# First part of a fused two-branch residual block: four unread products ahead of the first transposes, the first weight's rounding moved from ScalarE to VectorE, and two projections placed next to each other

## The chip, the cores and the metric

The kernel runs on one core of one Trainium2 chip. The metric is the device time of one execution in microseconds (us). The kernel before took 925.51 us, the median of three runs that lie between 925.22 and 925.88.

## The reference

The block normalises 1040 rows (16 learned rows ahead of 1024 frames, 1024 wide), projects them with one wide matrix, runs two branches on slices of the projection, merges them through gates, projects the result and normalises again. Cut to what matters here:

```python
h = concat([meta, x])                      # 1040 rows of 1024, padded
u = rmsnorm(h, norm_g)                     # what the first part forms
proj = u @ w_in                            # 1024 x 6144; its first pieces are formed in the first part
(sb_q, sb_k, sb_v, sb_gate, hg_q, hg_f, hg_i, hg_gate, gate_sb, gate_hg) = split(proj)
y_sb = stick_breaking(sb_q, sb_k, sb_v) * silu(sb_gate)
y_hg = group_rmsnorm(hgrn2(hg_q, hg_f, hg_i, lb)) * silu(hg_gate)
h = h + (sigmoid(gate_sb) * (y_sb @ w_sb_out) + sigmoid(gate_hg) * (y_hg @ w_hg_out)) @ w_out
out = rmsnorm(h, final_norm_g)[16:1040]
```

## The kernel before

Every operand of a large product is kept as two rounded parts, a high part and a low part that holds what the rounding left, and a product is formed as high x high + low x high + high x low. `uh` and `ul` are the two parts of the normalised rows, transposed so that channels lie on the partitions; `wh` and `wl` those of a weight of 1024 x 128.

The change lies in the first part. It takes the rows in nine blocks of 128 (the last has 16), brings each into `uh` and `ul`, and between them forms projections for three of the four `hg_i` weights, in pieces of 256 columns (the last 272). All instructions of ScalarE, VectorE and TensorE in this part stand in an order that is written out by hand, a table of short step names that is worked off from left to right; each engine then runs its own instructions strictly in that order. GpSimd and the SyncE queue, which issues the loads, follow their program order and wait on semaphores. The steps, with the engine and the line of the profile:

- `S b`: sum of squares of block b (ScalarE, L169). `r b`: its inverse root (GpSimd, L175). `D b`: the block scaled (VectorE, L181; in two halves for blocks 0 and 1).
- `T b k`: four transposes of 128 x 128 of half k of block b (TensorE, L189), into one of two buffers in PSUM called `tr` for even b, or of two called `z` for odd b.
- `H b k`: rounds that half into `uh` (ScalarE, L198). `L b k`: the low part into `ul` (VectorE, L202). `R b k`: an unrounded copy into `xb` (ScalarE, L208). A buffer in PSUM is free again when its H, L and R are done, so `T30` waits for `R10`, `T50` for `R30`, `T60` for `R40`.
- `w i`: the high parts of weight i, four instructions of 128 x 256 (ScalarE, L330). `v i c`: a quarter of its low parts (VectorE, L335).
- `P i q`: the piece q of projection i, 24 products (TensorE, L345): eight of `uh` with `wh`, eight of `ul` with `wh`, eight of `uh` with `wl`. Piece 0 needs blocks 0 and 1, piece 1 blocks 2 and 3, and so on. `E i q`: its copy out of PSUM (ScalarE, L315) and a store issued on ScalarE's queue (L316).
- `X`, `Y`, `y`, `Z`: later sums of the blocks (VectorE and ScalarE, L219 to L222 and L353 to L361).

After the table comes the fourth `hg_i` projection (L259, products of 348 and 346 columns), and after that everything else.

Of the kernel before, what the change touches and what calls it, by code (L numbers as in the profile page):

```python
# [9 lines left out]
F32R = mybir.dt.float32r  # L10
# [5 lines left out]
P = 128  # L16
D = 1024
NC = D // P
SEQ = 1024
NM = 16  # L20
L = SEQ + NM
# [6 lines left out]
SH = 2  # L28
# [17 lines left out]
def block_kernel(ctx: ExitStack, tc: tile.TileContext, x, meta, norm_g, w_in, w_sb_out,  # L46
                 w_hg_out, w_out, hg_norm_g, hg_lb_logits, final_norm_g, out):
    nc = tc.nc
    V, S, G, T = nc.vector, nc.scalar, nc.gpsimd, nc.tensor
# [5 lines left out]
    def nm(s):  # L55
        uid[0] += 1
        return f"{s}_{uid[0]}"
# [7 lines left out]
    def sb(tag, shape, dt=F32):  # L65
        p = base if tag in HOME else here[-1]
        return p.tile(shape, dt, tag=tag, name=nm(tag), bufs=BUFS.get(tag, 1))

    def ps(tag):
        return psum.tile([P, 512], F32, tag=tag, name=nm(tag), bufs=PB[tag])  # L70
# [7 lines left out]
    ident = sb("ident", [P, P])  # L78
# [14 lines left out]
    def fetch_w(src, col, chunks):  # L93
        if chunks > NC // 2:
            raw = sb("wr", [P, NC, P])
        else:
            if not half_rows:
                t = sb("wl", [P, 2, NC // 2, P])
                half_rows.extend((t[:, 0], t[:, 1]))
            half_rows.reverse()  # L100
            raw = half_rows[0]
        nc.sync.dma_start(raw[:, :chunks], src[:, col:col + P].rearrange("(c p) n -> p c n", p=P))
        return raw
# [30 lines left out]
    start = ExitStack()  # L134
# [11 lines left out]
    w3 = SUM[4][0].rearrange("p (a c) (d n) -> p a (c d) n", a=2, n=P)  # L146
    xbs, raws, eps_x = [], [], []
# [175 lines left out]
    first_w = {}  # L323

    def high_w(i):
# [3 lines left out]
        for c in range(0, NC, SH):  # L329
            S.activation(h[:, c:c + SH], raw[:, c:c + SH], AF.Copy)  # L330

    def low_w(i, c):
        h, lo = first_w[i]
        cs = slice(c * SL, c * SL + SL)
        V.tensor_tensor(lo[:, cs], raws[i][:, cs], h[:, cs].bitcast(F32), op=ALU.subtract)  # L335
        if c == 3 and i == 0:
            raws.append(fetch_w(w_in[0], FIRST[2], NC))
# [21 lines left out]
    def further_low(b, k):  # L359
        src, h, low, ts = FURTHER[b, k]  # L360
        formed["low"] = V.tensor_tensor(low[:, :, ts], src, h[:, :, ts].bitcast(F32), op=ALU.subtract)  # L361


    STEPS = dict(S=stats, r=root, D=scaled, T=turned, H=high_part, L=low_part, R=whole, w=high_w, v=low_w, P=piece, E=kept_piece, X=further,
                 Y=further_high, y=further_high_s, Z=further_low)
    with tc.manual_schedule(engines={mybir.EngineType.Activation, mybir.EngineType.DVE, mybir.EngineType.PE}):
        for step in """
            S0 S1 w0 r0 D0 T00 H00 r1 T01 H01 D1 T10 H10 L00 T11 H11 S2 R00 L01 R01 S3 w1
            L10 L11 v00 v01 v02 v03 P00 r2 D2 T20 H20 r3 T21 H21 R10 R11 S4 D3 v10 v11 v12 v13
            P10 L20 T30 H30 L21 T31 H31 E00 R20 R21 S5 E10 w2 r4 D4 L30 L31 P01 v20 T40 H40 v21  # L370
            T41 H41 E01 R30 R31 S6 v22 P11 v23 r5 D5 T50 H50 L40 T51 H51 S7 E11 R40 L41 P20 R41
            r6 D6 T60 H60 L50 T61 H61 E20 R50 L51 P21 R51 S8 E21 r7 P02 D7 T70 H70 X0 T71 H71
            Y02 P12 Z02 L60 R60 L61 R61 E02 r8 D8 T80 H80 X1 T81 H81 Y12 P22 Z12 L70 R70 L71 R71
            L80 R80 L81 P03 R81 E12 E22 y01 y11 E03 X2 P13 y21 Y22 P23 Z22 X3 y31 Y32 Z32 X4 y41
            E13 y03 y13 E23 y23 y33 y43 y04 y14 y24 y34 y44 Y42 Z42 Z01 Z11 Z21 Z31 Z41 Z03 Z13 Z23
            Z33 Z43 Z04 Z14 Z24 Z34 Z44
            """.split():
            STEPS[step[0]](*(int(n) for n in step[1:]))
    lbl = sb("lbl", [P, 2, 4])
# [647 lines left out]
    for p in range(4):  # L1027
        for hh in range(2):
            u = [Unit(pairs[p][0], hh, g, g % 2) for g in range(4)]
# [270 lines left out]
```

## Time and profile before

| what | value |
|---|---|
| median of three runs | 925.51 us |
| the profiled execution | 926.64 us |
| its span, first to last instruction | 924.9 us |
| TensorE busy in the span | 899.3 us (97%) |
| VectorE, ScalarE, GpSimd busy | 659.2, 397.3, 267.8 us |
| the first part: first product of the table to first product of L259 | 8.07 to 57.57 us |

Rows of the timeline give the start in us, the duration, the engine, the line, the operation, what is written and read, how many instructions were merged, and in brackets how long the engine had stood idle before and what ended that. Rows of stretches give for each engine the busy time in the stretch. A matmul's record overlaps the next one, so the distance between starts is the pace and the duration of a merged row is a little longer than what it occupies.

### The profile page before, as it was taken

How to read it: one execution, taken by the hardware profiler on the slowest of the kernel's cores; microseconds unless marked ns; L12 is line 12 of the kernel's file. 1: busy time of each engine (PE TensorE's matmuls, PEld its weight loads, DVE VectorE, ACT ScalarE, POOL GpSimd, SP SyncE). 2: the span in 40 equal slices, each digit the busy share in tenths (PEclk: the TensorE clock that was granted, in tenths of full speed). 3: DMA queues.
4: the chain of work that ended last, by engine and by line, in shares of the span. 5: the costliest groups of instructions: out<-in, count | busy, mean ns of one | idle time of the engine just before them, and what ended most of it. 6: DMA issues, size and time to landing. Idle time of an engine off the chain costs nothing.

```text
span 924.9 us, 13722 instructions
## 1 busy us (share of the span) xinstructions
PE 899.3 (97%) x5000; PEld 781.8 (85%) x5000; DVE 659.2 (71%) x1205; ACT 397.3 (43%) x909; POOL 267.8 (29%) x285
## 2 busy tenths in 40 slices
PE   7999999999999999999999999999999999999996
PEld 6998888888889998898898888898978888888885
DVE  6893456554423477888788788868687887997886
ACT  6763334333333455555555555232324154323341
POOL 2026445544432211132111221424332000003552
PEclk9999999999999999999999999999999999999999
DMA  8223543333336122221141132131111347564212
GB/s 275 65 68 102 169 137 103 125 106 122 103 126 188 53 81 79 69 69 58 58 115 57 58 92 85 43 102 58 58 57 47 103 142 268 187 224 156 94 46 92
DMA packets 90581, 98.03 MB, mean 106 GB/s; under 512 B 6017, under 2 KB 65281, under 8 KB 90514
## 3 DMA queue, kind: packets, MB, share of 16 engines
q1 hardware_dynamic: 76688, 73.52, 26.0%
q10 hardware_dynamic: 13826, 23.64, 6.9%
q8 instruction: 40, 0.66, 0.3%
q14 instruction: 27, 0.22, 0.1%
HBM read 71.94 MB, written 25.20 MB: 105 GB/s over the span
## 4 chain that ended last, share of the span: by engine, by line
PE 80%; DVE 10%; ACT 4%; issue 2%; DMA 2%; POOL 1%; SPq 0%; ACTq 0%; DVEq 0%; POOLq 0%
PE acc L259 31%; PE acc L461 10%; PE z L461 7%; PE tr L461 7%; PE acc L1227 4%; PE av L677 3%; PE z L833 3%; PE tr L663 2%; PE z L621 2%; PE z L1227 2%; PE tr L1227 2%; PE acc L345 2%; DVE ab L630 2%; DVE ab L626 1%; DMA wr<-in_w_in 1%
## 5 line engine op out<-in xcount | busy, mean ns | idle before, releaser
L259 PE MATMUL acc<-uh,wh 128*128 128x346 f32 (+2 forms) x472 | 173.4, 367 | 0.0
L259 PE MATMUL acc<-uh,wl 128*128 128x346 f32 (+2 forms) x472 | 165.4, 350 | 0.0
L259 PE MATMUL acc<-ul,wh 128*128 128x346 f32 (+2 forms) x472 | 165.2, 350 | 0.0
L120 POOL TENSOR_TENSOR wl<-wr,wh 128x256 fp32r<-128x256 f32 x92 | 74.9, 836 | 300.4 <-ACT wh L115 272.8
L259 PEld LDWEIGHTS acc<-uh,wl 128*128 128x128 f32 x472 | 89.0, 189 | 6.0
L259 PEld LDWEIGHTS acc<-uh,wh 128*128 128x128 f32 x472 | 89.2, 189 | 3.6
L259 PEld LDWEIGHTS acc<-ul,wh 128*128 128x128 f32 x472 | 89.4, 189 | 2.5
L450 POOL TENSOR_TENSOR pw<-su,pw 128x512 fp32r<-128x512 f32 x44 | 59.2, 1366 | 44.2 <-ACT pw L449 44.0
L623 ACT ACTIVATE ab<-z 128x456 f32<-128x456 f32 (+6 forms) x112 | 49.9, 448 | 30.6 <-PE z L621 30.3
L450 POOL TENSOR_TENSOR pw<-wr,pw 128x512 fp32r<-128x512 f32 x33 | 43.7, 1325 | 61.2 <-ACT pw L449 61.2
L666 DVE TENSOR_TENSOR wt<-tr,wt 128x512 fp32r<-128x512 f32 (+1 forms) x80 | 50.4, 631 | 13.9 <-ACT wt L665 12.2
L626 DVE TENSOR_TENSOR_SCAN ab<-ab,later 128x456 f32<-128x456 f32 (+3 forms) x64 | 54.8, 858 | 6.8 <-ACT ab L623 6.1
L461 PE MATMUL acc<-th,pw 128*128 128x512 f32 x176 | 58.1, 391 | 0.0
L677 PE MATMUL av<-wt,v 128*128 128x256 f32 x320 | 53.9, 287 | 3.6 <-DVE wt L666 2.0
L665 ACT ACTIVATE wt<-tr 128x512 fp32r<-128x512 f32 (+1 forms) x80 | 44.2, 554 | 29.3 <-PE tr L663 29.0
L621 PE MATMUL z<-stk,q 128*128 128x456 f32 (+6 forms) x224 | 56.7, 334 | 0.0
L842 DVE COPY_PREDICATED ab<-mask,z 128x192 f32<-128x192 uint8 (+2 forms) x144 | 45.2, 352 | 13.0 <-PE z L833 11.6
L677 PEld LDWEIGHTS av<-wt,v 128*128 128x128 f32 x320 | 46.9, 188 | 8.4 <-DVE wt L666 3.7
L630 DVE TENSOR_TENSOR_SCAN ab<-ab 128x348 f32<-128x348 f32 (+4 forms) x48 | 46.9, 976 | 7.6 <-ACT ab L623 6.2
L449 ACT ACTIVATE pw<-su 128x512 fp32r<-128x512 f32 x44 | 25.8, 625 | 60.9 <-DVE su L444 36.8
L663 PE MATMUL tr<-ident,ab 128*128 128x128 f32 x288 | 45.0, 273 | 0.0
L115 ACT ACTIVATE wh<-wr 128x256 fp32r<-128x256 f32 x92 | 33.8, 411 | 26.0 <-issue 15.2
(348 smaller groups left out, 2107.1 us busy)
## 6 DMA issues: line engine op xcount, KB each, us to landing
wr<-in_w_in SPq DMA_DIRECT2D x48, 512.0 KB, 4.2
q<-q SPq DMA_DIRECT2D x32, 256.0 KB, 4.3
wr<-in_w_out SPq DMA_DIRECT2D x16, 512.0 KB, 3.9
sg<-gate SPq DMA_DIRECT2D x24, 256.0 KB, 4.0
gate<-sg ACTq DMA_DIRECT2D x20, 256.0 KB, 2.0
xb<-in_x SPq DMA_DIRECT2D x7, 512.0 KB, 8.7
gate<-co ACTq DMA_DIRECT2D x12, 256.0 KB, 2.0
pt<-hi SPq DMA_DIRECT2D x4, 520.0 KB, 3.1
```

Source lines behind the costliest of these rows:

```text
L120: eng.tensor_tensor(lo[:, cs], raw[:, cs], h[:, cs].bitcast(F32), op=ALU.subtract)
L259: T.matmul(acc, a, b, start=(k == 0), stop=(k == total - 1))
L450: G.tensor_tensor(t[:, 1], d[key], t[:, 0].bitcast(F32), op=ALU.subtract)
L461: T.matmul(acc, t[:, part // 2, c], (bh, bl, bh)[part][:, c], start=(c == part == 0), stop=(c == 3 and part == 2))
L621: T.matmul(z, qt[:, k, qo + qi * P:qo + (qi + 1) * P], st["k"][hh][:, c0:c1], start=(k == 0), stop=(k == 1))
L623: S.activation(a[:, c0:c1], z, AF.Sigmoid, scale=-1.0)
L626: ins = V.tensor_tensor_scan(w, w, later[:, WS - (n - c0):][:, ::-1], 1.0, op0=ALU.mult, op1=ALU.max)
L630: V.tensor_tensor_scan(w, w, w, a[:, c1:c1 + 1], op0=ALU.mult, op1=ALU.bypass)
L663: T.transpose(tp[:, c:c + P], self.w[qi][:, s0:s0 + P], ident)
L666: V.tensor_tensor(wt[:, 1, lo:], tp[:, lo:], wt[:, 0, lo:].bitcast(F32), op=ALU.subtract)
L677: T.matmul(self.av, st["v"][hh][:, 2 * gg + j], wt[:, part, where[j]:where[j] + 256], start=(gg == g and part == 0 and j == 0), stop=False)
L1227: T.matmul(acc, t[:, part // 2, c], (bh, bl, bh)[part][c], start=(c == part == 0), stop=(c == 3 and part == 2))
```

## The change

Three things change, all in the first part.

1. A new step `K4` between `r0` and `D0` issues four products of the identity with itself into a PSUM buffer called `av` that nothing reads.
2. The high parts of the first weight are formed by VectorE (`u0`, after `D1` and `T10`) and no longer by ScalarE (`w0`, which stood ahead of `H00`).
3. The table is written in another order: `P10` follows directly on `P00`, ahead of the transposes of block 2; `L10` goes ahead of `L01`; the scaling `D3` goes behind the low parts `v10` to `v13`; `S4` goes behind `H31`; `L30` and `L31` go ahead of `D4`.

```diff
+    def high_w_g(i):
+        raw = raws[i]
+        h, lo = (w3[:, 0], w3[:, 1]) if i == 2 else (sb("wh", [P, NC, P], F32R), sb("wl", [P, NC, P], F32R))
+        first_w[i] = h, lo
+        for c in range(0, NC, SH):
+            V.tensor_copy(h[:, c:c + SH], raw[:, c:c + SH])
+
+    def keep_busy(n):
+        idle = ps("av")
+        for _ in range(n):
+            T.matmul(idle[:, :P], ident, ident, start=True, stop=True)
...
-            S0 S1 w0 r0 D0 T00 H00 r1 T01 H01 D1 T10 H10 L00 T11 H11 S2 R00 L01 R01 S3 w1
-            L10 L11 v00 v01 v02 v03 P00 r2 D2 T20 H20 r3 T21 H21 R10 R11 S4 D3 v10 v11 v12 v13
...
+            S0 S1 r0 K4 D0 T00 H00 r1 T01 H01 D1 T10 H10 u0 T11 H11 S2 L00 R00 L10 L01 R01
+            w1 S3 L11 v00 v01 v02 v03 P00 r2 D2 v10 v11 v12 v13 P10 r3 T20 H20 D3 T21 H21 R10
...
```

The new lines push the later code down by 13, so L345 of before is L358 after, and L335 is L348.

TensorE from the first transposes to block 2. Each row is one instruction or several alike: the line, the operation, what is written and read, the size and the count; `acc_206` is `P00` and `acc_257` is `P10` before. Before:

```order
L189 MATMUL tr_153<-ident_63,xb_98 128x128 x4
L189 MATMUL tr_160<-ident_63,xb_98 128x128 x4
L189 MATMUL z_168<-ident_63,xb_102 128x128 x4
L189 MATMUL z_175<-ident_63,xb_102 128x128 x4
L345 MATMUL acc_206<-uh_72,wh_144 128x256 x8
L345 MATMUL acc_206<-ul_73,wh_144 128x256 x8
L345 MATMUL acc_206<-uh_72,wl_145 128x256 x8
L189 MATMUL tr_233<-ident_63,xb_107 128x128 x4
L189 MATMUL tr_240<-ident_63,xb_107 128x128 x4
L345 MATMUL acc_257<-uh_72,wh_192 128x256 x8
L345 MATMUL acc_257<-ul_73,wh_192 128x256 x8
L345 MATMUL acc_257<-uh_72,wl_193 128x256 x8
```

The same place on TensorE after the change, where `acc_211` is `P00` and `acc_242` is `P10`:

```order
L343 MATMUL av_145<-ident_63 128x128 x4
L189 MATMUL tr_152<-ident_63,xb_98 128x128 x4
L189 MATMUL tr_159<-ident_63,xb_98 128x128 x4
L189 MATMUL z_167<-ident_63,xb_102 128x128 x4
L189 MATMUL z_179<-ident_63,xb_102 128x128 x4
L358 MATMUL acc_211<-uh_72,wh_173 128x256 x8
L358 MATMUL acc_211<-ul_73,wh_173 128x256 x8
L358 MATMUL acc_211<-uh_72,wl_174 128x256 x8
L358 MATMUL acc_242<-uh_72,wh_194 128x256 x8
L358 MATMUL acc_242<-ul_73,wh_194 128x256 x8
L358 MATMUL acc_242<-uh_72,wl_195 128x256 x8
L189 MATMUL tr_268<-ident_63,xb_107 128x128 x4
```

The four products on the identity come first, and the 24 products of `P10` now stand between `P00` and the first transposes of block 2 (`tr_268`, before `tr_233`).

VectorE in the same place, from the scaling of block 1 (`xb_102`) to that of block 3 (`xb_110`). Before:

```order
L181 SCALAR_TENSOR_TENSOR xb_102<-xb_102,s_37_141,gbc_90 128x512 x2
L202 TENSOR_TENSOR ul_73<-tr_153,uh_72 128x4x128
L202 TENSOR_TENSOR ul_73<-tr_160,uh_72 128x4x128
L202 TENSOR_TENSOR ul_73<-z_168,uh_72 128x4x128
L202 TENSOR_TENSOR ul_73<-z_175,uh_72 128x4x128
L335 TENSOR_TENSOR wl_145<-wr_105,wh_144 128x256 x4
L181 SCALAR_TENSOR_TENSOR xb_107<-xb_107,s_46_182,gbc_90 128x1024
L181 SCALAR_TENSOR_TENSOR xb_110<-xb_110,s_49_189,gbc_90 128x1024
L335 TENSOR_TENSOR wl_193<-wr_113,wh_192 128x256 x4
```

The same place on VectorE after the change:

```order
L181 SCALAR_TENSOR_TENSOR xb_102<-xb_102,s_37_141,gbc_90 128x512 x2
L337 CAST wh_173<-wr_105 128x256 x4
L202 TENSOR_TENSOR ul_73<-tr_152,uh_72 128x4x128
L202 TENSOR_TENSOR ul_73<-z_167,uh_72 128x4x128
L202 TENSOR_TENSOR ul_73<-tr_159,uh_72 128x4x128
L202 TENSOR_TENSOR ul_73<-z_179,uh_72 128x4x128
L348 TENSOR_TENSOR wl_174<-wr_105,wh_173 128x256 x4
L181 SCALAR_TENSOR_TENSOR xb_107<-xb_107,s_47_186,gbc_90 128x1024
L348 TENSOR_TENSOR wl_195<-wr_113,wh_194 128x256 x4
L181 SCALAR_TENSOR_TENSOR xb_110<-xb_110,s_52_201,gbc_90 128x1024
```

Four casts now stand ahead of the low parts of blocks 0 and 1, and the low parts of the second weight stand ahead of the scaling of block 3.

ScalarE from the high parts of block 2 (`uh_72<-tr_233`) to the first copy out (`sg_296<-acc_206`, `E00`). Before:

```order
L198 ACTIVATE uh_72<-tr_233 128x4x128
L198 ACTIVATE uh_72<-tr_240 128x4x128
L208 ACTIVATE xb_102<-z_168 128x512
L208 ACTIVATE xb_102<-z_175 128x512
L169 ACTIVATE sq_250,s_57_248<-xb_115 128x1025
L198 ACTIVATE uh_72<-z_283 128x4x128
L198 ACTIVATE uh_72<-z_290 128x4x128
L315 ACTIVATE sg_296<-acc_206 128x256
```

The same place on ScalarE after the change:

```order
L198 ACTIVATE uh_72<-tr_268 128x4x128
L198 ACTIVATE uh_72<-tr_275 128x4x128
L208 ACTIVATE xb_102<-z_167 128x512
L208 ACTIVATE xb_102<-z_179 128x512
L198 ACTIVATE uh_72<-z_284 128x4x128
L198 ACTIVATE uh_72<-z_291 128x4x128
L169 ACTIVATE sq_299,s_61_297<-xb_115 128x1025
L315 ACTIVATE sg_301<-acc_211 128x256
```

The same eight instructions stand there; the sum of squares of block 4 (`xb_115`) moved from ahead of the high parts of block 3 to behind them.

More of the change, by code (lines that the diff above doesn't have):

```diff
@@ L361, in further_low @@
         formed["low"] = V.tensor_tensor(low[:, :, ts], src, h[:, :, ts].bitcast(F32), op=ALU.subtract)
-    STEPS = dict(S=stats, r=root, D=scaled, T=turned, H=high_part, L=low_part, R=whole, w=high_w, v=low_w, P=piece, E=kept_piece, X=further,
+    STEPS = dict(S=stats, r=root, D=scaled, T=turned, H=high_part, L=low_part, R=whole, w=high_w, u=high_w_g, K=keep_busy, v=low_w, P=piece, E=kept_piece, X=further,
                  Y=further_high, y=further_high_s, Z=further_low)
@@ L367, in block_kernel @@
         for step in """
-            S0 S1 w0 r0 D0 T00 H00 r1 T01 H01 D1 T10 H10 L00 T11 H11 S2 R00 L01 R01 S3 w1
-            L10 L11 v00 v01 v02 v03 P00 r2 D2 T20 H20 r3 T21 H21 R10 R11 S4 D3 v10 v11 v12 v13
[L370 to L376, printed above, removed]
+            S0 S1 r0 K4 D0 T00 H00 r1 T01 H01 D1 T10 H10 u0 T11 H11 S2 L00 R00 L10 L01 R01
+            w1 S3 L11 v00 v01 v02 v03 P00 r2 D2 v10 v11 v12 v13 P10 r3 T20 H20 D3 T21 H21 R10
+            R11 L20 T30 H30 L21 T31 H31 S4 E00 R20 R21 S5 E10 w2 L30 L31 P01 r4 D4 T40 H40 v20
+            T41 H41 E01 R30 R31 S6 v21 P11 v22 v23 r5 D5 T50 H50 L40 T51 H51 S7 E11 R40 L41 P20
+            R41 r6 D6 T60 H60 L50 T61 H61 E20 R50 L51 P21 R51 S8 E21 r7 P02 D7 T70 H70 X0 T71
+            H71 Y02 P12 Z02 L60 R60 L61 R61 E02 r8 D8 T80 H80 X1 T81 H81 Y12 P22 Z12 L70 R70 L71
+            R71 L80 R80 L81 P03 R81 E12 E22 y01 y11 E03 X2 P13 y21 Y22 P23 Z22 X3 y31 Y32 Z32 X4
+            y41 E13 y03 y13 E23 y23 y33 y43 y04 y14 y24 y34 y44 Y42 Z42 Z01 Z11 Z21 Z31 Z41 Z03 Z13
+            Z23 Z33 Z43 Z04 Z14 Z24 Z34 Z44
             """.split():
```

## The prediction

> **What bounds the kernel now.** I read the page first: how full TensorE is, and the chain that ended last.
>
> ```profile
> span 924.9 us, 13722 instructions
> PE 899.3 (97%) x5000; PEld 781.8 (85%) x5000; DVE 659.2 (71%) x1205; ACT 397.3 (43%) x909; POOL 267.8 (29%) x285
> PE 80%; DVE 10%; ACT 4%; issue 2%; DMA 2%; POOL 1%; SPq 0%; ACTq 0%; DVEq 0%; POOLq 0%
> ```
>
> TensorE carries the span, so a change in the first part is worth what it moves TensorE's last piece there. The next view is the busy time by stretches, cut at the steps of the first part.
>
> ```profile
> core 0: us, PE busy (x) PEld busy (x) DVE busy (x) ACT busy (x) POOL busy (x), PEclk, DMA share, GB/s
> 12.30:17.19 4.89, 4.89 (x25) 4.89 (x26) 4.45 (x9) 4.70 (x11) 1.49 (x2) 1.00 1.04 385
> 17.19:34.57 17.38, 15.90 (x131) 14.91 (x129) 12.41 (x21) 14.50 (x32) 2.19 (x4) 1.00 0.46 118
> 34.57:57.57 23.00, 23.00 (x193) 22.77 (x193) 22.11 (x38) 13.53 (x34) 4.15 (x5) 1.00 0.12 40
> 57.57:917.20 859.63, 847.98 (x4638) 734.93 (x4636) 611.46 (x1127) 357.24 (x819) 255.88 (x253) 1.00 0.32 103
> ```
>
> From T60 (34.57) on TensorE has no gap until L259 starts at 57.57: whatever T60 is late or early arrives there unchanged. Later TensorE idles 11.6 us in 860, with VectorE behind the longest entry of the waits, work that is itself fed by TensorE, so it shifts along:
>
> ```profile
> PE z L833 <- DVE ab L842: 2.5, 4, 1.0
> ```
>
> So the question is when T60 starts. The timeline of TensorE:
>
> ```profile
> 2.35 3.75 PE L142 MATMUL acc<-gbc,sg 1*128 1x512 f32 x4 [2.35 <-DMA gbc<-in_norm_g]
> 8.07 1.97 PE L189 MATMUL tr<-ident,xb 128*128 128x128 f32 x8 [1.98 <-DVE xb L181]
> 9.95 1.97 PE L189 MATMUL z<-ident,xb 128*128 128x128 f32 x8
> 12.30 2.08 PE L345 MATMUL acc<-uh,wh 128*128 128x256 f32 x8 [0.39 <-ACT uh L198]
> 14.18 1.91 PE L345 MATMUL acc<-ul,wh 128*128 128x256 f32 x8
> 15.88 1.47 PE L345 MATMUL acc<-uh,wl 128*128 128x256 f32 x8
> 17.19 1.04 PE L189 MATMUL tr<-ident,xb 128*128 128x128 f32 x8
> 17.98 1.19 PE L345 MATMUL acc<-uh,wh 128*128 128x256 f32 x8
> 19.01 1.10 PE L345 MATMUL acc<-ul,wh 128*128 128x256 f32 x8
> 19.95 1.11 PE L345 MATMUL acc<-uh,wl 128*128 128x256 f32 x8
> 20.89 1.03 PE L189 MATMUL z<-ident,xb 128*128 128x128 f32 x8
> 34.57 1.14 PE L189 MATMUL tr<-ident,xb 128*128 128x128 f32 x8 [0.86 <-ACT xb L208]
> ```
>
> Two things stand out. Until about 16.6 TensorE runs at half pace: eight transposes take 1.97 us and later 1.04; eight products of 256 columns take 1.70 (14.18 to 15.88, 0.213 each) and later 0.94 (19.01 to 19.95, 0.117 each). The column for the granted clock reads 1.00 all the while, so this gate is seen in durations only. And T60 waited for ScalarE (R40). ScalarE's and VectorE's rows:
>
> ```profile
> 9.46 1.34 ACT L330 ACTIVATE wh<-wr 128x256 fp32r<-128x256 f32 x4 [1.55 <-DMA wr<-in_w_in]
> 10.70 1.06 ACT L198 ACTIVATE uh<-tr 128x512 fp32r<-128x512 f32 x2
> 15.64 1.36 ACT L330 ACTIVATE wh<-wr 128x256 fp32r<-128x256 f32 x4
> 17.82 1.09 ACT L198 ACTIVATE uh<-tr 128x512 fp32r<-128x512 f32 x2 [0.82 <-PE tr L189]
> 18.80 1.10 ACT L208 ACTIVATE xb<-z 128x512 f32<-128x512 f32 x2
> 19.75 1.09 ACT L169 ACTIVATE sq<-xb 128x1025 bf16<-128x1025 f32 x1
> 21.53 1.09 ACT L198 ACTIVATE uh<-z 128x512 fp32r<-128x512 f32 x2 [0.61 <-PE z L189]
> 22.50 0.39 ACT L315 ACTIVATE sg<-acc 128x256 f32<-128x256 f32 x1
> 33.92 1.08 ACT L208 ACTIVATE xb<-tr 128x512 f32<-128x512 f32 x2 [0.41 <-DVE ul L202]
> ```
>
> ```profile
> 9.14 1.42 DVE L181 SCALAR_TENSOR_TENSOR xb<-xb,s,gbc 128x512 f32<-128x512 f32 x2 [0.46 <-POOL s L175]
> 11.31 1.29 DVE L202 TENSOR_TENSOR ul<-tr,uh 128x512 fp32r<-128x512 f32 x2 [0.76 <-ACT uh L198]
> 13.71 1.42 DVE L335 TENSOR_TENSOR wl<-wr,wh 128x256 fp32r<-128x256 f32 x4
> 15.05 1.28 DVE L181 SCALAR_TENSOR_TENSOR xb<-xb,s,gbc 128x1024 f32<-128x1024 f32 x1
> 38.06 0.39 DVE L353 CAST th<-xb 128x448 fp32r<-128x448 f32 x1
> 57.25 0.19 DVE L353 CAST th<-xb 128x64 fp32r<-128x64 f32 x1
> ```
>
> From H20 at 17.82 to R40 at 33.92 ScalarE is the pacemaker: 14.50 us of its work lie in 17.38, and most of the rest are the slots of about 0.4 in which its queue issues the stores behind each E. It only really waits 0.61 us, ahead of H30. So T60 hangs on when H20 starts and on how much ScalarE waits after that.
>
> **The change part by part.** K4: L142's two products of 512 columns hold TensorE 3.75 us, so one of 128 columns costs a quarter of half of that, 0.47, and four 1.9. They can start at 6.10 and end by 8.0, inside the 1.98 us in which TensorE waits for D0 ahead of T00 at 8.07. Price 0; the cover is that wait. Were they 0.3 longer, T00 and P00's start would slip, but P00's end is set elsewhere (next). Ends: 0 and +0.3 for T00, 0 for the sum.
>
> u0 for w0: ScalarE loses 1.34 us and H00, which stood behind it until 10.70, can follow T00 at about 9.3. VectorE gains four casts. Between 0.19 (64 columns) and 0.39 (448) one of 256 is 0.29; issued back to back with the overlap of L335's rows (four of 0.42 in 1.42, so 0.34 apart and 0.08 over) they hold VectorE 0.8; the ends are 0.5 and 1.3. D1 ends at 10.56, and VectorE stood idle there for 0.76, waiting for H00. The casts fill that hole: L00 starts at 11.3 as before, the four L and the four v take 3.8, and v03 ends at 15.1 as before (9.14 to 15.13 is one row of work without a hole). So the low parts that P00 needs last come no sooner.
>
> P00: it starts behind T11 at 11.7 instead of 12.30. If the gate opens by about 13.3, its third group waits for v03 at 15.1 and ends at 15.46, 1.7 earlier than 17.19. This is all that the earlier gate can bring: VectorE, not TensorE, then sets P00's end.
>
> P10 ahead of T20: 24 products at 0.117 are 2.8 us, from 15.46 to 18.27. Its own inputs are there: w1 runs on ScalarE from 14.4 (the load, below, had landed), v1 from 16.2 to 17.7. T20 so starts at 18.27 instead of 17.19, and H20, 0.64 behind T20 (17.19 to 17.82), at 18.91: +1.08. ScalarE, which has nothing before H20 but S3 until 16.9, stands idle 2 us, so the 1.34 us taken off it are lost there.
>
> S4 behind H31, and P10's place: before, from H20 to E00 ScalarE takes 4.68 (17.82 to 22.50), of which 0.61 is the wait for T30, which stood behind P10. After, T30 needs the `z` buffer that R10 frees. R10 is now behind H20: 18.91 + 0.98 (two H) + 0.60 = 20.5, so TensorE idles from 19.2 to 20.5, T30 lands H30 at 21.25, and ScalarE, free at 20.86, waits 0.4 instead of 0.61. Two H, S4 (1.04) and E00 comes at 23.3: +0.8. From E00 to R40 the order on ScalarE is the same, so T60 is +0.8 late.
>
> The rest: T40 needs D4, behind S4 (23.3), GpSimd's root (0.55 below) and D4 (1.28), so 25.4, no later than before; T50 waits for R30 anyway. D3 behind v13 ends at 18.9, ahead of 20.5. The third weight's load is released by v03 as before, the fourth's by v13 at 17.7 instead of 19.4; SyncE has nothing else behind them. Price 0 each. Its bound on the second weight: issued at 4.18, landed at most 9.6 later, 13.8.
>
> ```profile
> 4.18 0.45 SPq L102 DMA_DIRECT2D wr<-in_w_in x1
> DMA to landing us min/median/max: 4.1/5.1/9.6
> 21.06 0.55 POOL L175 TENSOR_TENSOR s<-s,mhalf 128x1 f32<-128x1 f32 x1 [4.33 <-ACT sq L169]
> ```
>
> Sum: P00 -1.7, P10 ahead of T20 +2.8 (H20 +1.08), ScalarE's shorter wait and S4 -0.3: +0.8 us, with 0.4 either way from the casts. The profiled execution took 926.64 around its span of 924.9 and so would take 927.4; it stands 1.1 above the median of 925.51, and against that I get 926.3.
>
> **The rivals.** *The gate stays late (B).* Nothing shows that K4 opens it. The rows show two stretches of dense work that did not: L142's 3.75 us, and T10 to the first products (9.95 on, one gap of 0.39). It opened after 4.3 us of products alone. If transposes do not count, K4's 1.9 us ahead of them do nothing, P00 runs 24 x 0.213 = 5.1 us at half pace from 11.7 and ends at about 16.8; P10 ends at 19.6, H20 starts at 20.2 (+2.4), T60 is 2.1 late: 927.6. For it: P00's half pace right behind sixteen transposes. Against: in the order after, TensorE has hardly a gap from 8.07 on.
> The Trainium skill, "TensorE: Matmul & The Clock Gate", part 4 on the transpose by TensorE, says that transposes do not count as busy for the gate in the same way; by that this rival holds, and the sum would be +2.1 instead of +0.8. The trace does not contradict it (16 transposes ran at half pace), but the same page's window of about 3.4 us, which by its part 1 runs freely, would explain the rows too.
>
> *ScalarE is not the pacemaker (C), the other side.* If R30 and R40 came as early as TensorE could use them, its idle 1.48 us between 17.19 and 34.57 would vanish, and P10 (2.9 there, 17.98 to 20.89) is done already. T60 then starts at 18.27 + 17.38 - 2.9 - 1.5 = 31.3, 3.3 early: 922.2. It decides from T60 at 32.7 (1.85 us early) on. Against it: ScalarE would need to do in 12.4 us what it has 16 us of rows for.
>
> *No net effect (D).* The gate opens at another moment in each run (the runs before spread over 0.66 us), and where before it opened later than in this profile, the +0.8 shrinks: 925.5 to 925.8.
>
> **How the numbers follow.** No change that can be told from none is within 0.2%, 1.85 us. A, gate by 13.3: 0.50, at 926.3, own range 925.8 to 927.0. B: 0.30, at 927.6, two thirds of it beyond 927.36. D: 0.12. C: 0.08. Faster 0.08; slower 0.20 from B and 0.05 from A's tail and D's, 0.25; same 0.67. The range leaves out C and a little of B's top: 925.0 to 928.2.
>
> **What would show it.** Four `av` products between 6.1 and 8.0, T00 still at 8.07. The pace of the products of P00: 0.117 from its second group on (A), or 0.213 to about 16.6 (B). VectorE without a hole from 9.14 to v03's end at 15.1. T20 at about 18.3 (A) or 19.6 (B). A new wait of TensorE of 1.3 us ahead of T30 on R10 (ScalarE, L208). E00 at 23.3, T60 at 35.4, L259 at 58.4. It is wrong if H20 starts before 17.8, or if ScalarE's rows between E00 and R40 shrink.

## The result: 3.2 us slower, and the profile after

The changed kernel took 928.62 us against 925.40 (medians of six runs each): 1.0031 of before, interval 1.0020 to 1.0041, so 1.9 to 3.8 us more. I had said 926.3, in 925.0 to 928.2. The profiled execution took 928.35 with a span of 926.6.

TensorE's timeline in the first part, after:

```profile
6.02 2.08 PE L343 MATMUL av<-ident 128*128 128x128 f32 x8
8.64 1.97 PE L189 MATMUL tr<-ident,xb 128*128 128x128 f32 x8 [0.55 <-DVE xb L181]
10.40 1.91 PE L189 MATMUL z<-ident,xb 128*128 128x128 f32 x8
12.15 1.58 PE L358 MATMUL acc<-uh,wh 128*128 128x256 f32 x8
13.57 1.23 PE L358 MATMUL acc<-ul,wh 128*128 128x256 f32 x8
14.64 1.28 PE L358 MATMUL acc<-uh,wl 128*128 128x256 f32 x8
15.75 1.11 PE L358 MATMUL acc<-uh,wh 128*128 128x256 f32 x8
18.58 1.04 PE L189 MATMUL tr<-ident,xb 128*128 128x128 f32 x8
20.84 1.15 PE L189 MATMUL z<-ident,xb 128*128 128x128 f32 x8 [1.23 <-ACT xb L208]
25.82 1.06 PE L189 MATMUL tr<-ident,xb 128*128 128x128 f32 x8 [0.53 <-DVE xb L181]
30.81 1.14 PE L189 MATMUL z<-ident,xb 128*128 128x128 f32 x8 [1.11 <-ACT xb L208]
35.62 0.55 PE L189 MATMUL tr<-ident,xb 128*128 128x128 f32 x3 [0.86 <-ACT xb L208]
```

P00 ends at 15.75, P10 follows without a gap, and the transposes of block 2 start at 18.58. Ahead of T30 stands the new wait of 1.23 on R10, ahead of T50 one of 1.11 on R30. ScalarE and VectorE after:

```profile
16.07 1.07 ACT L169 ACTIVATE sq<-xb 128x1025 bf16<-128x1025 f32 x1
19.22 1.09 ACT L198 ACTIVATE uh<-tr 128x512 fp32r<-128x512 f32 x2 [1.99 <-PE tr L189]
20.19 1.09 ACT L208 ACTIVATE xb<-z 128x512 f32<-128x512 f32 x2
21.54 1.09 ACT L198 ACTIVATE uh<-z 128x512 fp32r<-128x512 f32 x2 [0.26 <-PE z L189]
22.52 1.06 ACT L169 ACTIVATE sq<-xb 128x1025 bf16<-128x1025 f32 x1
23.56 0.38 ACT L315 ACTIVATE sg<-acc 128x256 f32<-128x256 f32 x1
```

```profile
10.49 0.89 DVE L337 CAST wh<-wr 128x256 fp32r<-128x256 f32 x4
11.30 0.68 DVE L202 TENSOR_TENSOR ul<-tr,uh 128x512 fp32r<-128x512 f32 x1
13.93 1.42 DVE L348 TENSOR_TENSOR wl<-wr,wh 128x256 fp32r<-128x256 f32 x4
```

K4's row counts 8, since each of its four products left two records. ScalarE stands idle for 1.99 ahead of H20, E00 comes at 23.56. The casts hold VectorE 0.8 (10.49 to 11.30), v03 ends at 15.35. All of this is case A of the prediction within 0.4 us, but for T00, 0.57 late with the rows of the first block (S0 at 6.02, before at 5.45). Against the first profile of before T60 is 1.05 late and the last product 1.73. The other 0.7 arises at 731, where ScalarE waited 7.3 instead of 6.0 for the load of `w_sb_out`; that is no cost of the change, since the same wait is 7.4 in the second profile of before (e1) and lies between 6.0 and 7.6 in all fourteen profiles. That leaves 1.5 of the 3.2 unexplained by these two profiles: the question was what the first profile of before had that usual runs have not.

### The profile page after: what moved, and what is told of

It reads as the page before. It is cut to its first block, busy times and chain, and to the rows that moved or that the text cites. A ratio compares the mean times of both kernels' runs of the same rounds, so it can differ in the third digit from the quotient of the medians.

```text
span 926.6 us, 13739 instructions
## 1 busy us (share of the span) xinstructions
PE 899.8 (97%) x5008; PEld 781.0 (84%) x5008; DVE 660.8 (71%) x1209; ACT 396.8 (43%) x905; POOL 267.5 (29%) x285
## 4 chain that ended last, share of the span: by engine, by line
PE 80%; DVE 10%; ACT 4%; DMA 2%; issue 2%; POOL 1%; SPq 0%; ACTq 0%; DVEq 0%; POOLq 0%
PE acc L259 30%; PE acc L474 10%; PE z L474 7%; PE tr L474 7%; PE acc L1240 4%; PE av L690 3%; PE z L846 3%; PE z L634 2%; PE tr L676 2%; PE tr L1240 2%; PE z L1240 2%; PE acc L358 2%; DVE ab L643 2%; DVE ab L639 1%; DVE wt L679 1%
## 5 line engine op out<-in xcount | busy, mean ns | idle before, releaser
L259 PE MATMUL acc<-uh,wh 128*128 128x346 f32 (+2 forms) x472 | 173.0, 367 | 0.0
L259 PE MATMUL acc<-uh,wl 128*128 128x346 f32 (+2 forms) x472 | 165.2, 350 | 0.0
L259 PE MATMUL acc<-ul,wh 128*128 128x346 f32 (+2 forms) x472 | 164.9, 349 | 0.0
L259 PEld LDWEIGHTS acc<-uh,wl 128*128 128x128 f32 x472 | 88.8, 188 | 6.0
L259 PEld LDWEIGHTS acc<-uh,wh 128*128 128x128 f32 x472 | 89.0, 188 | 3.6
L259 PEld LDWEIGHTS acc<-ul,wh 128*128 128x128 f32 x472 | 89.2, 189 | 2.6
L679 DVE TENSOR_TENSOR wt<-tr,wt 128x512 fp32r<-128x512 f32 (+1 forms) x80 | 50.4, 631 | 13.9 <-ACT wt L678 12.3
L855 DVE COPY_PREDICATED ab<-mask,z 128x192 f32<-128x192 uint8 (+2 forms) x144 | 45.3, 352 | 12.7 <-PE z L846 11.4
L462 ACT ACTIVATE pw<-su 128x512 fp32r<-128x512 f32 x44 | 25.9, 626 | 60.0 <-DVE su L457 35.4
```

The source lines that it names most:

```text
L259: T.matmul(acc, a, b, start=(k == 0), stop=(k == total - 1))
L679: V.tensor_tensor(wt[:, 1, lo:], tp[:, lo:], wt[:, 0, lo:].bitcast(F32), op=ALU.subtract)
```

## The experiments

Each ratio is to the kernel before on the same chip; its medians in the three series were 925.78, 926.01 and 925.67. Listed are the moment at which the trace's clock record puts the end of the half pace, and the start of T60; times in us from the span's start. That record begins with the first stretch at full pace, and the profile's column for the clock counts what lies ahead of it as full.

| kernel | median | ratio, interval | half pace ends | T60 |
|---|---|---|---|---|
| before, first profile | | | 16.7 | 34.57 |
| e1 before again | 926.01 | 1.0001, 0.9992 to 1.0009 | 12.3 | 33.25 |
| e2 K4 alone | 925.55 | 0.9997, 0.9988 to 1.0006 | 11.1 | 32.93 |
| changed | 928.62 | 1.0031, 1.0020 to 1.0041 | 12.5 | 35.62 |
| e3 changed without K4 | 928.01 | 1.0023, 1.0014 to 1.0032 | 11.4 | 35.49 |
| e4 R10, R11, S4 early, misplaced | 933.83 | 1.0082, 1.0069 to 1.0096 | 11.6 | 41.24 |
| e5 R10, R11, S4 early | 926.13 | 1.0001, 0.9992 to 1.0010 | 9.7 | 32.91 |
| e6 the order alone | 927.83 | 1.0022, 1.0013 to 1.0031 | 14.3 | 35.87 |
| e7 S4 alone | 929.29 | 1.0036, 1.0024 to 1.0049 | 13.4 | 36.99 |
| e8 u0 alone | 927.05 | 1.0012, 1.0003 to 1.0021 | 12.8 | 33.79 |
| e9 P10 alone | 928.35 | 1.0029, 1.0019 to 1.0039 | 11.5 | 35.71 |
| e10 before, later load | 927.00 | 1.0017, 1.0008 to 1.0026 | 16.0 | 34.33 |
| e11 changed, later load | 928.70 | 1.0032, 1.0019 to 1.0044 | 11.6 | 35.37 |
| e12 filled order | 923.90 | 0.9979, 0.9970 to 0.9988 | 14.1 | 33.98 |

**e1, the kernel before again.** No edit that issues an instruction.

> The kernel before once more, with the new helper functions in the file and neither of them called. Both theories: the time stays within 0.1% of 925.4. It is run for its second profile: if first-part theory alone is right, this profile shows TensorE's rows in the first part as in the first profile (gate open at about 16.6, T60 at 34.6) and the span of 924.9 was about 1 us above the usual for reasons after 57.6; if the gate's moment wanders from run to run, T60 lies up to 0.7 us earlier than 34.57.

TensorE's timeline of this second profile of before:

```profile
9.82 1.97 PE L189 MATMUL z<-ident,xb 128*128 128x128 f32 x8
11.63 1.59 PE L358 MATMUL acc<-uh,wh 128*128 128x256 f32 x8
13.06 1.10 PE L358 MATMUL acc<-ul,wh 128*128 128x256 f32 x8
14.00 1.10 PE L358 MATMUL acc<-uh,wl 128*128 128x256 f32 x8
15.83 1.07 PE L189 MATMUL tr<-ident,xb 128*128 128x128 f32 x8 [0.73 <-ACT wh L330]
19.56 1.03 PE L189 MATMUL z<-ident,xb 128*128 128x128 f32 x8
33.25 1.15 PE L189 MATMUL tr<-ident,xb 128*128 128x128 f32 x8 [0.84 <-ACT xb L208]
```

ScalarE and VectorE of the same profile:

```profile
8.33 1.34 ACT L330 ACTIVATE wh<-wr 128x256 fp32r<-128x256 f32 x4 [0.55 <-DMA wr<-in_w_in]
9.57 1.06 ACT L198 ACTIVATE uh<-tr 128x512 fp32r<-128x512 f32 x2
16.59 1.08 ACT L198 ACTIVATE uh<-tr 128x512 fp32r<-128x512 f32 x2
21.17 0.39 ACT L315 ACTIVATE sg<-acc 128x256 f32<-128x256 f32 x1
```

```profile
10.35 1.28 DVE L202 TENSOR_TENSOR ul<-tr,uh 128x512 fp32r<-128x512 f32 x2
13.07 1.42 DVE L348 TENSOR_TENSOR wl<-wr,wh 128x256 fp32r<-128x256 f32 x4
14.40 1.28 DVE L181 SCALAR_TENSOR_TENSOR xb<-xb,s,gbc 128x1024 f32<-128x1024 f32 x1
```

This answers most of the question. Here w0 starts at 8.33 and not at 9.46, H00 follows 1.1 earlier, P00 starts straight behind the transposes at 11.63, and the half pace ends within its first group. P00 is over at 15.0 instead of 17.2. T20 then waits for the scaled block 2: the bracket names w1, but in e1, e2 and e8 alike T20 starts 0.15 after D2 ends (15.68 here). T60 starts at 33.25 instead of 34.57.

Two things keep this from being the whole answer. The last product of e1 is only 0.46 earlier than in the first profile, since that one had the shorter wait for `w_sb_out`, 6.0 against 7.4. And a late first weight is no rarity: in the twelve profiles whose kernel issues this load in the same place, the last of its sixteen parts landed between 8.30 (e1) and 9.44 (first profile), in four of them after 9.0. From here on I compare with e1: the changed kernel's T60 is 2.37 late and its last product 2.19.

**e2 and e3, K4 alone and the change without it.**

```diff
-            S0 S1 w0 r0 D0 T00 ...
+            S0 S1 w0 r0 K4 D0 T00 ...       (e2, on before)
-            S0 S1 r0 K4 D0 T00 ...
+            S0 S1 r0 D0 T00 ...             (e3, on the change)
```

> The kernel before with only the four unread products (K4 behind r0). Theory 1 (K4 opens the gate): half pace ends at about 12.5 instead of 16.6, P00 ends on VectorE's low parts (v03 at 15.1, then the last products) at 16.4, T20 0.8 earlier, T60 at 33.9, time 0.7 us less than before, 924.7. Rival (K4 does nothing, the gate opens because products follow densely): half pace to about 16.6, T60 34.6, 925.4.

> The changed kernel without the four unread products. Theory 1 (K4 opens the gate): half pace until 15.5 to 17, P00 ends at about 16.8, T20 at 19.6, T60 1.1 to 1.4 later than in the changed kernel, 929.9. Rival (dense transposes and products open it, K4 does nothing): pace, T20 (18.6) and time (928.6) as in the changed kernel.

Theory 1 (K4 opens the gate) falls in e3: without K4 the half pace ended at 11.4, as early as with it, T20 came at 18.46, and the time (928.01) lies with the changed kernel's 928.62, their intervals overlapping. In e2 both theories had the wrong starting point, since the gate opens early in e1 as well: T60 is 0.3 earlier than in e1, and the interval of the time includes no change. K4 neither brings nor costs time that these runs can tell. It may still move the gate: the two earliest ends of the half pace, 9.7 in e5 and 11.1 in e2, are of kernels with K4.

**e4 and e5, ScalarE's hole filled.** R10, R11 and S4 go into the 2 us ahead of H20. In e4 they stood ahead of L11 in the table.

```diff
-            ... w1 S3 L11 v00 ... H20 D3 T21 H21 R10 R11 L20 T30 H30 L21 T31 H31 S4 E00 ...
+            ... w1 S3 S4 R10 R11 L11 v00 ... H20 D3 T21 H21 L20 T30 H30 L21 T31 H31 E00 ...    (e4)
+            ... w1 S3 L11 R10 R11 S4 v00 ... H20 D3 T21 H21 L20 T30 H30 L21 T31 H31 E00 ...    (e5)
```

> The changed kernel with three steps of ScalarE, R10, R11 and S4, put ahead of H20, into the 2 us in which ScalarE stands idle there. Theory 1 (ScalarE's chain from H20 to R40 sets T60): TensorE's wait ahead of T30 goes, T30 at 19.3 instead of 20.8, E00 at 21.1 instead of 23.6, T60 2.4 us earlier than in the changed kernel (33.2), time 926.2. Rival (the loss sits after 57.6, in loads that land at another moment): T60 moves as said but the time stays at about 928.6, or moves by less than half of it.

TensorE in e4:

```profile
19.78 1.23 PE L358 MATMUL acc<-ul,wh 128*128 128x256 f32 x4 [5.79 <-DVE ul L202]
20.81 1.91 PE L358 MATMUL acc<-uh,wl 128*128 128x256 f32 x8
```

L11 reads the same PSUM buffer as R11, and with R11 ahead of it in the table L11 waited until R11 was done, at 19.0 (VectorE stood idle for 5.50 ahead of L11, by its row behind L208). TensorE stood still for 5.79 in the middle of P00, and after that it ran at half pace again (eight products in 1.7). The run missed its aim and says nothing on the theories; it shows, for this one pair, that a step's place in the table is also its place in the line for a buffer.

> The changed kernel with R10, R11 and S4 ahead of H20 on ScalarE, but behind L11 in the table (in the run before, L11 of VectorE waited for R11, because the two read the same PSUM buffer and R11 stood first). Theory 1 (ScalarE's chain from H20 to R40 sets T60): no wait ahead of T30, T30 at 19.3, E00 at 21.1, T60 at 33.1 to 33.3, 2.4 earlier than in the changed kernel, time 925.5 to 926. Rival (the loss sits after 57.6, in loads that land later): T60 moves but the time stays at about 928.

TensorE in e5:

```profile
9.89 1.07 PE L189 MATMUL z<-ident,xb 128*128 128x128 f32 x8
19.21 1.06 PE L189 MATMUL z<-ident,xb 128*128 128x128 f32 x8 [0.16 <-DVE xb L181]
32.91 1.14 PE L189 MATMUL tr<-ident,xb 128*128 128x128 f32 x8 [0.86 <-ACT xb L208]
```

As expected by theory 1: T30 at 19.21, T60 2.7 earlier than in the changed kernel (0.6 of it stands already at T20, 18.01 against 18.58), and the time back at that of before, between 0.7 less and 0.9 more. The loss came through ScalarE's late chain from H20 to R40, and it is had back at ScalarE.

**e6, e7, e9 and e8, the parts alone.** The new order with w0 on ScalarE and no K4:

> The new order alone: no K4, and the first weight's high parts on ScalarE again (w0). Theory 1 (the order costs nearly all): T20 at 18.1 to 18.6, a wait ahead of T30, T60 at 35.3 to 35.8, time 927.7 to 928.3. Rival (the four casts on VectorE cost most of it): T60 below 34.3, time at most 926.6.

The time is 1.2 to 2.9 us longer and T60 comes at 35.87, in a profile whose S0 started 0.7 later than in e1 (5.99 and 5.30). Theory 1 holds as far as the intervals can tell: the order alone costs most of the loss. Within it, P10 ahead of T20 on the kernel before:

```diff
-            ... P00 r2 D2 T20 H20 r3 T21 H21 R10 R11 S4 D3 v10 v11 v12 v13 P10 L20 T30 ...
+            ... P00 r2 D2 v10 v11 v12 v13 P10 T20 H20 r3 T21 H21 R10 R11 S4 D3 L20 T30 ...
```

> The kernel before with P10 and its low parts v10 to v13 ahead of T20 and D3 behind them; w0, S4 and the rest as before, no K4. Theory 1 (H20, and with it ScalarE's chain to R40, waits for 24 products more): T20 at 18.5 to 19.2 instead of 15.8, a wait ahead of T30 on R10, E00 2.4 and T60 2.4 later than in the second profile of before, time 928.3. Rival (P10 has to be done anyway and later waits give it back): T60 within 0.8 of 33.3, time below 926.8.

```profile
19.05 1.03 PE L189 MATMUL tr<-ident,xb 128*128 128x128 f32 x8
21.32 1.15 PE L189 MATMUL z<-ident,xb 128*128 128x128 f32 x8 [1.23 <-ACT xb L208]
35.71 0.55 PE L189 MATMUL tr<-ident,xb 128*128 128x128 f32 x3 [0.60 <-ACT xb L208]
```

T20 comes 3.2 later than in e1, the wait ahead of T30 is there, T60 is 2.46 late and the time 2.7 longer (1.8 to 3.6): this one move gives as much as the whole change.

S4 behind H31 on the kernel before:

```diff
-            ... R10 R11 S4 D3 ... H31 E00 ...
+            ... R10 R11 D3 ... H31 S4 E00 ...
```

> The kernel before with one step moved: S4 from ahead of H30 to behind H31. Theory 1: in the old place S4 lies in ScalarE's wait for T30 and costs nothing, in the new one it delays E00 and all of ScalarE behind it by 1.0, and D4 and T40 with it: E00 at 22.2 instead of 21.2, T60 1.6 later than in the second profile of before (34.9), time 927.4. Rival (ScalarE catches up, since it waits elsewhere before R40): T60 within 0.4 of 33.3, time 925.8 to 926.1.

```profile
25.50 1.34 PE L358 MATMUL acc<-ul,wh 128*128 128x256 f32 x8 [2.92 <-DVE ul L202]
28.02 1.91 PE L189 MATMUL tr<-ident,xb 128*128 128x128 f32 x8
32.91 1.03 PE L189 MATMUL z<-ident,xb 128*128 128x128 f32 x8
```

T60 is 3.74 late instead of 1.6. About 0.5 of that was there before S4's move could act: the first weight came late in this profile too (w0 at 9.34), and T20 stood at 16.35 instead of 15.83. In the old order D4, which needs S4, stands ahead of L30 and L31 on VectorE, so TensorE waited 2.92 inside P01 for L30, and afterwards ran at half pace for 3.4 us (eight transposes 1.91, then 1.03). The changed kernel has L30 and L31 ahead of D4, so this is not S4's price there; that price I have only together with R10's and R11's, in e5.

u0 on VectorE on the kernel before:

```diff
-            S0 S1 w0 r0 D0 ... T10 H10 L00 ...
+            S0 S1 r0 D0 ... T10 H10 u0 L00 ...
```

> The kernel before with u0 on VectorE instead of w0 on ScalarE, nothing else. Theory 1: where the first weight lands at 8.3 as in the second profile, VectorE has a hole of only 0.2 between D1 and L00 and the casts put v03's end 0.5 to 0.6 later, at 15.1: T60 0.5 later than 33.2, time 926.3. Rival of the prediction (the casts fill a hole of 0.8): v03's end and T60 as in before, time 925.8.

GpSimd's root of block 2 in e8:

```profile
13.53 1.39 POOL L175 TENSOR_TENSOR s<-s,mhalf 128x1 f32<-128x1 f32 x1 [5.13 <-DVE wl L348]
```

T60 is 0.54 late, as expected, but not by the way expected: v03 ended at 14.5 as in e1, since D1 here followed D0 without a gap, and T20 was late behind D2, which waited for a root that took 1.39 instead of 0.6. The time is 0.3 to 1.9 us longer. That u0 alone costs is measured; by which way in a usual run stays open.

**e10 and e11, a later first weight.** Its load goes behind that of block 2.

```diff
-        if b in (1, 3):
-            raws.append(fetch_w(w_in[0], FIRST[b // 2], NC))
+        if b in (2, 3):
+            raws.append(fetch_w(w_in[0], FIRST[b - 2], NC))
```

> The kernel before with the load of the first weight issued behind that of block 2 instead of ahead of it. Theory 1 (before, the first weight's landing lies on the path through w0 and H00, and the first profile had caught a late one): w0 starts 1 us or more later than 8.35, at 9.4 to 10.4, the order and TensorE's rows look like the first profile, T60 0.5 to 1.5 later than 33.25, time 926.5 to 927.5. Rival (the landing does not matter): T60 at 33.3, 926.0.

ScalarE and TensorE in e10:

```profile
9.59 1.34 ACT L330 ACTIVATE wh<-wr 128x256 fp32r<-128x256 f32 x4 [2.04 <-DMA wr<-in_w_in]
```

```profile
12.43 2.07 PE L345 MATMUL acc<-uh,wh 128*128 128x256 f32 x8 [0.79 <-ACT uh L198]
14.30 1.85 PE L345 MATMUL acc<-ul,wh 128*128 128x256 f32 x8
```

With the load put late the first profile comes again: w0 at 9.6, a gap ahead of P00, half pace to 16.0, T60 at 34.33, and 0.7 to 2.4 us more.

> The changed kernel with the same later load. Theory 1 (u0 comes on VectorE only behind D1, at about 10.5, and so has room for a landing up to then): T60 within 0.3 of the changed kernel's 35.6, time 928 to 928.7. Rival (the landing matters there as well): T60 1 us later, 929.5.

The changed kernel does not mind (T60 at 35.37 and 35.62; ratios 1.0032 and 1.0031). u0 does take the load off the path. But where the load comes as in e1, P00 follows the transposes without a gap, so there was little to win, and e8 shows what u0 costs.

**e12, an order built on this.** From e5's: w0 back on ScalarE, K4 out, and three moves that give TensorE products while ScalarE frees its buffers.

```diff
-            ... P11 v22 v23 r5 D5 T50 H50 L40 T51 H51 S7 E11 R40 L41 P20 R41 r6 D6 T60 H60 L50 T61 H61 E20 R50 L51 P21 R51 ...
+            ... P11 v22 v23 P21 r5 D5 S7 T50 H50 L40 T51 H51 E11 R40 L41 P20 R41 r6 D6 E20 T60 H60 L50 T61 H61 R50 L51 R51 ...
```

> An order built on the findings: the new order with w0 on ScalarE and no K4, R10, R11 and S4 ahead of H20, P21 ahead of T50, S7 ahead of the transposes of block 5, and E20 ahead of those of block 6, so that TensorE has products while ScalarE frees the buffers. Theory 1: T30 at 19.0, no wait of TensorE over 0.3 from P10 to P23, L259 at 53.5 to 54.2 instead of 56.2 in the second profile of before, time 923.2 to 924. Rival (the later part gives an earlier start back): L259 comes earlier but the time stays within 0.1% of before.

TensorE's timeline and its only wait between 12 and 56:

```profile
26.52 1.11 PE L358 MATMUL acc<-uh,wl 128*128 128x256 f32 x8
27.47 1.10 PE L358 MATMUL acc<-uh,th 128*128 128x256 f32 x8
30.27 1.04 PE L189 MATMUL z<-ident,xb 128*128 128x128 f32 x8
33.98 1.04 PE L189 MATMUL tr<-ident,xb 128*128 128x128 f32 x8
54.05 0.32 PE L259 MATMUL acc<-uh,wh 128*128 128x348 f32 x1
```

```profile
PE acc L358 <- ACT uh L198: 0.4, 1, 0.4
```

L259 starts at 54.05 (56.20 in e1), the last product is 2.3 earlier, and the time is 0.9979 of before, 1.1 to 2.8 us less: a version that beats both.

## Why the prediction was wrong

By its own steps:

- **The term that failed is "P00 -1.7".** It took P00's end of before, 17.19, for what T20 waits for. That profile had caught a late first weight (w0 at 9.46; 8.33 in e1) and a late end of the half pace (16.7; 12.3 in e1); that the first caused the second is not shown. In e1 P00 ends at 15.0, and T20 waits for D2 until 15.83. In the changed kernel P00 ends at 15.75, so the term was worth 0.1 and not 1.7, and P10's 2.8 was set off by next to nothing: H20 16.59 to 19.22 is +2.63, less 0.24 that ScalarE saves to E00 (4.58 to 4.34; I had said 0.3), gives E00 +2.39 and T60 +2.37. The sum should have been +2.4, and 927.9 sits in the measured interval; the runs can't tell the 0.8 to the median from noise.
- **The sign was there to read.** The profiled execution was 1.1 above the median, with runs within 0.66 of each other. I moved the level by it and did not ask which row held the 1.1. How much of it the late weight was stays open: by the medians of e10 a late one costs 0.7 to 2.4, but the profiled executions of the two profiles of before, 926.64 and 926.12, are only 0.5 apart.
- **"The casts fill that hole"** leaned on the same late load. The hole of 0.76 on VectorE ahead of L00 was the load's; e1 shows none to speak of. u0 alone costs 0.3 to 1.9 us.
- **That the 1.34 us taken off ScalarE are lost** was right, the place was not: with w0 still on ScalarE (e6) it stands idle for 2.28 ahead of H20, without w0 for 1.99. What w0 left free went into 1.54 us of waiting for T00 ahead of H00.
- **K4 at 0 was right**, and so was that an earlier gate brings nothing beyond VectorE's v03 (15.1 said, 15.35 measured). In e2, P00 is over at 14.6 and T20 starts only at 15.5.
- **The chain behind P00 was right**: ScalarE's idle 2 us (1.99), the wait ahead of T30 (1.3; 1.23), E00 (23.3; 23.56), T60 (35.4; 35.62), L259 (58.4; 58.57), with the first block loaded 0.6 later than before. Against the first profile T60 came 1.05 later, with +0.8 said; the chain was reckoned well, and the level that it was set against was not the usual one. The later work shifted along as said, but for the wait at 731, whose 6.0 to 7.6 moves the end by about 1 us from run to run.
- **Rival B fell.** The Trainium skill, "TensorE: Matmul & The Clock Gate", part 4, has it that transposes do not count as busy for the gate in the same way. No trace here bears that out for these f32 transposes: in e5 the transposes of block 1 already run at full pace (eight in 1.07) with only one-row products, K4 and transposes ahead, and in e3 the half pace ended at 11.4 with nothing but transposes since 7.97. The window that the prediction set beside it, about 3.4 us, is in the clock records (below).
- **Rival D had the right cause and the wrong sign**: the gate does wander, 9.7 to 16.7 over these profiles, but the first profile of before was the latest of them all.
- **Rival C** did not happen by itself, but e12 shows that such time was there: TensorE's waits between P10 and L259 go when its products are put where ScalarE is late.

## What to carry to other kernels

When a profiled execution lies above the median of the runs, find the row that holds the difference before crediting an edit with curing it; a second profile of the same kernel is worth more than any argument on the first. A move that puts 2.8 us of ready work ahead of a short step pays only if nobody waits for that step: here sixteen us of another engine's strictly ordered work hung on eight transposes. Work taken off an engine is worth something only where that engine is late; the 1.3 us taken off ScalarE reappeared as waiting for T00 ahead of H00.

## What the runs showed of the hardware

- The clock changes on a grid of 3.413 us: in the fourteen clock records every stretch that ends within the record is a whole multiple of it (1, 2, 4, 261, and 265 to 267 times). Where the grid lies differs from run to run.
- If the grid is drawn back from the end of the half pace, the gate opened each time at the end of a grid stretch filled with products of 128 rows, transposes among them. Twelve of the fourteen such stretches had at most 0.18 idle. Stretches filled without a gap by one-row products did not open it (2.85 to 6.27 in e5, 3.20 to 6.61 in e7).
- A short gap is not shown to decide it: stretches with 0.42 (e4) and 0.45 (e7) idle opened, one with 0.39 (first profile, 9.85 to 13.26) did not, nor one with 0.79 (e10), and there the half pace lasted one grid stretch longer, to 16.7 and 16.0. No run varied the gap by itself.
- One stall is enough to close the gate: after 2.92 us (e7) and 5.79 us (e4) of TensorE standing still, products ran at half pace once more, for 3.4 us in e7; the waits of up to 1.23 in the changed kernel did not do it.
- The same root of 128 x 1 on GpSimd took from 0.55 to 1.39 us, the latter while VectorE was busy on the low parts. What lengthens it was not tried.
- The same load of 512 KB in the same place of the queue had landed at 8.30 and at 9.44 in two executions of one kernel; in the late one 14 of its 16 parts were there by 8.26.
